# The first chunk of a latent projection on un-normed x, x read in two parts, modulation pieces in pairs

## The chip, the cores and the metric

The kernel runs on one core of one Trainium2 chip, in one launch. The metric is the device time of that launch in microseconds (us). Three runs of the kernel before took 2443.82, 2444.87 and 2444.91 us; the median, 2444.87 us, is the time before.

## The reference, cut to what matters

The program is one step of a two-layer trunk on 640 tokens (512 latent tokens from `x_sample`, 128 context tokens from `x_prompt`), each with 2048 features. The change lies in the first steps of the first layer, which compute this:

```python
def modulate_and_norm(x, cond, w_mod, b_mod, g):
    m = (jax.nn.silu(cond) @ w_mod + b_mod)[:, None, :]
    shift, scale, gate = jnp.split(m, 3, axis=-1)
    return rmsnorm(x, g) * (1 + scale) + shift, gate
...
h, g = modulate_and_norm(xp, cond_ctx, mod_w_ab[j], mod_b_ab[j], norm_ab[j])   # xs with c
...
q_lat, kv_lat, k_pe, a_gate, b_q, b_ff, b_fb, b_i, b_gate = split_cols(h @ w_in, AB_SIZES)
```

`rmsnorm(x, g)` is x · R · g, with R one number for each token: the inverse root of the mean square over all 2048 features. `w_mod` is 2048 x 6144 in float32, and of its columns shift takes 0 to 2047 and scale 2048 to 4095. Of `h @ w_in` the first stage computes the first 832 columns (the latent columns) and two gate blocks of 128.

## The kernel before

Activations stand transposed: features on the 128 partitions, the 640 tokens along the free axis, so 2048 features are 16 tiles, k = 0 to 15. TensorE (PE) multiplies float32 in three products: `split` makes a high and a low part of an operand (ACT writes the high part, DVE the low one), and `three` (lines 113 to 115) issues high·high, high·low and low·high.

The scheduler places every instruction by times of its own and writes one fixed order for each engine; an engine takes its instructions in that order and waits for semaphores. Nearly every DMA is issued by SyncE's queue (SP), also in one fixed order. It is the start stage (`run`, the block with the pool `start`) that the change rewrites:

- `conditioning` makes silu of the two conditions (`sc`).
- `read_x` reads the whole of x by rows of tokens: four tiles `x` of 128 tokens x 2048 (1 MB each), and the prompt in two tiles of the pool `rawp`. ACT squares each block of 512 for the sums of squares (line 372), PE transposes it in 128 x 128 blocks (line 48), and DVE copies the blocks to `xT`. For each group of 128 tokens, R is found and spread over the partitions by a small matmul (line 384).
- `start` needs scale and shift of tile k before it can build the operand `h[k]`. A column group j of `w_mod` (256 columns, thus two tiles k) is read as four pieces of 4 x 128 x 256 (512 KB each) into `rawp`; PE multiplies a piece in four column groups at a time (`mod_tensor`, line 269), then a copy (`modrow`) and a small matmul (line 277) put the result on the partitions. Block b needs the groups j = 8 + b (scale) and j = b (shift), so eight pieces and two small matmuls. All 16 groups (64 pieces, 33.6 MB) pass in this stage.
- `modulate(k)` multiplies tile k of `xT` by R (line 432), applies scale and shift (line 434) and splits the result into `act`.
- `columns(k0, k1, c)` multiplies a chunk of k tiles by column group c of `w_in_ab` (nine groups; a weight tile of two k is 128 KB), in two halves of 320 tokens, thus 12 matmuls for two k; the sums are gathered in `lat`, on ACT for the first chunk (line 411) and on DVE for the others (line 413). The chunks are k 0-1, 2-3, 4-7, 8-11 and 12-15, and while a chunk is multiplied, the pieces for the next chunks are multiplied between its matmuls.

`rawp` has four buffers, so that at most four pieces are loaded or loading. PSUM has four buffers `w` for transposes and small products, two `m` for the pieces and two `acc` for the matmuls of `columns`. In names as `raw_409` or `acc_521` the number tells tiles of one kind apart.

Of the kernel before, what the change touches and what calls it, by code (L numbers as in the profile page):

```python
# [14 lines left out]
P = 128  # L15
# [13 lines left out]
class Trunk:  # L29
# [229 lines left out]
    def mod_tensor(self, l, js):  # L259

        nc = self.nc
        wm = self.io[f"mod_w_{l}"][0].rearrange("(k p) c -> p k c", p=P)
        for j in js:
            ps = self.w("m")[:, :256]
            for kq in range(4):
                raw = self.t(self.rawp, [P, 4, 256], tag="raw")
                nc.sync.dma_start(raw, wm[:, 4 * kq:4 * kq + 4, 256 * j:256 * j + 256])
                for g in range(4):
                    nc.tensor.matmul(ps[32 * g:32 * g + 32, :], lhsT=self.sc[:, 4 * kq + g, :], rhs=raw[:, g, :],  # L269
                                     start=kq == 0, stop=kq == 3)  # L270
                if kq < 3:
                    yield
# [79 lines left out]
    def read_x(self, xin, sp):  # L352
# [4 lines left out]
        stats = []  # L357
        for i in range(5):
            if i < 4:
                x = self.t(xin, [P, D], tag="x", bufs=4)  # L360
                nc.sync.dma_start(x, io["x_sample"][0, P * i:P * i + P])
                blocks = [x[:, 512 * j:512 * j + 512] for j in range(4)]
            else:
                blocks = []
                for j in range(2):
                    x = self.t(self.rawp, [P, 1024], tag="raw")
                    nc.sync.dma_start(x, io["x_prompt"][0, :, 1024 * j:1024 * j + 1024])
                    blocks += [x[:, :512], x[:, 512:]]
            parts = self.t(sp, [P, 6], tag="parts", bufs=5)
            stats.append(parts)  # L370
            for j, x in enumerate(blocks):
                nc.scalar.activation(self.w("acc"), x, AF.Square, accum_out=parts[:, j:j + 1])
            for j, x in enumerate(blocks):
                p = self.w()
                for g in range(4):
                    self.transpose(p[:, P * g:P * g + P], x[:, P * g:P * g + P])
                nc.vector.tensor_copy(self.xblocks[j][:, :, P * i:P * i + P], p.rearrange("p (k t) -> p k t", t=P))
        for i, parts in enumerate(stats):
            r = self.t(sp, [P, 1], tag="r", bufs=2)
            nc.vector.reduce_sum(parts[:, 4:5], parts[:, 0:4], axis=AX.X)  # L380
            nc.vector.tensor_scalar(parts[:, 4:5], parts[:, 4:5], scalar1=1.0 / D, scalar2=None, op0=ALU.mult)
            self.rsqrt(r, parts[:, 4:5], parts[:, 5:6], EPS)
# [4 lines left out]
    def start(self):  # L387
        nc, io, sp = self.nc, self.io, self.startp
        self.h = []
        self.averages(sp, 1 / 512, 1 / 256)  # L390
        cols = [(P * c, P) for c in range(6)] + [(6 * P, 64)] + [(832 + P * h, P) for h in range(self.early)]
        sums = [self.t(sp, [P, T], tag="lat", bufs=len(cols)) for _ in cols]
        W = io["w_in_ab"][0].rearrange("(k p) c -> p k c", p=P)

        def columns(k0, k1, c):
# [3 lines left out]
            x = sums[c][:n]  # L399
            halves = [slice(HALF * h, HALF * h + HALF) for h in range(2)]  # L400
            done = []
            for s in halves:
                p = self.w("acc")[:n, :HALF]
                for k in range(k0, k1):
                    a = self.h[k]
                    self.three(p, (ws[:, 0, k - k0], ws[:, 1, k - k0]), (a[:, 0, s], a[:, 1, s]),
                               start=k == k0, stop=k == k1 - 1)
                done.append((s, p))
            for s, p in done:
                if k0 == 0:  # L410
# [17 lines left out]

        def modulate(k):
# [3 lines left out]
            for c, (s0, s1) in enumerate(((0, TS), (TS, T))):  # L433
                nc.vector.tensor_scalar(xn[:, s0:s1], xn[:, s0:s1], scalar1=self.mod["aba"][:, k, c:c + 1],
                                        scalar2=self.mod["ab"][:, k, c:c + 1], op0=ALU.mult, op1=ALU.add)
            a = self.t(self.act[k // 8], [P, 2, T + 2], F32R, tag="act")[:, :, 0:T]
            self.split(a[:, 0], a[:, 1], xn)
            self.h.append(a)

        work = []  # L440
        for b0, b1 in ((0, 1), (1, 2), (2, 4), (4, 6), (6, 8), (8, 8)):
            pieces = chain(*(self.mod_block(b, modulate) for b in range(b0, b1)))
            n = 8 * (b1 - b0)
            for j in range(4) if n == 0 else ():
                self.tc.keep_in_program_order(nc.sync.dma_start(
                    self.xT[4 * P * j:4 * P * (j + 1)].rearrange("(k p) t -> p k t", p=P), self.xblocks[j]))
# [6 lines left out]
            if b0 == 0:  # L453
                self.gains(sp)
            work = [lambda c=c, k0=2 * b0, k1=2 * b1: columns(k0, k1, c) for c in range(len(cols))]
# [505 lines left out]
    def out_ab(self, act, sp):  # L961
# [9 lines left out]
        for f in range(KT):  # L971
# [385 lines left out]
```

## Time and profile before

| | |
|---|---|
| runs | 2443.82, 2444.87, 2444.91 us (median 2444.87) |
| profiled execution | 2441.28 us, its span 2439.4 us, mean granted TensorE clock 0.995 |
| busy in the span | PE 2415.6 us (99%), DVE 1390.8 (57%), ACT 919.8 (38%), POOL 59.4 (2%) |
| DMA | 324.98 MB, 133 GB/s in the mean; 325 GB/s from 20 to 40 us |

The span runs from the first to the last instruction; the profiled execution's own time is 1.9 us longer and 3.6 us under the median. A busy PE is not PE at its peak: matmuls overlap, so the start of one after the other is the better measure of its pace. Instruction rows of the trace give start, length, engine, line, operation, output <- inputs and, in brackets, how long the engine stood idle before and what released it.

### The profile page before, as it was taken

The numbers are of one execution on the slowest core, as the hardware profiler recorded it, in microseconds if no ns is written. First come the engines' busy times: TensorE is split into PE (matmuls) and PEld (weight loads), VectorE is DVE, ScalarE is ACT, GpSimd is POOL, SyncE is SP. The second block draws the span as 40 slices with busy tenths as digits, with TensorE's granted clock in tenths as the row PEclk, the third lists the DMA queues.
The fourth block names the chain that finished last, engine by engine and source line by source line (L and its number), as shares of the span: only waits on it lengthen the run. The fifth ranks groups of instructions, "written<-read, shape, count | busy, mean of one in ns | idle before, by whom it ended". The sixth has DMA issues, their size and how long they took to land.

```text
span 2439.4 us, 42445 instructions
## 1 busy us (share of the span) xinstructions
PE 2415.6 (99%) x17418; PEld 2296.1 (94%) x17418; DVE 1390.8 (57%) x2874; ACT 919.8 (38%) x1717; POOL 59.4 (2%) x81
## 2 busy tenths in 40 slices
PE   7999999999999999999999999999999999999999
PEld 5789999999999999999999999999999999999999
DVE  5545455456455556566656668777765554654221
ACT  4314333333323333364544433443343443453121
POOL 1000000000000000000000121000000000000000
PEclk8999999999999999999999999999999999999999
DMA  9985544545545222453343655444432222225332
GB/s 313 307 260 153 168 146 149 164 132 164 157 126 153 71 65 73 137 147 92 91 118 107 192 170 160 128 118 123 132 115 72 75 81 78 74 66 162 115 113 61
DMA packets 396866, 324.98 MB, mean 133 GB/s; under 512 B 36250, under 2 KB 347968, under 8 KB 396160
## 3 DMA queue, kind: packets, MB, share of 16 engines
q1 hardware_dynamic: 396096, 322.17, 44.2%
q8 instruction: 137, 2.24, 0.4%
q0 software_dynamic: 576, 0.09, 0.1%
q14 instruction: 57, 0.47, 0.1%
HBM read 277.58 MB, written 36.76 MB: 129 GB/s over the span
## 4 chain that ended last, share of the span: by engine, by line
PE 95%; DMA 3%; DVE 1%; issue 0%; ACT 0%; SPq 0%; DVEq 0%; ACTq 0%
PE acc L113 25%; PE acc L115 24%; PE acc L114 24%; PE w L48 3%; PE o L1176 2%; PE m L292 2%; PE w L113 2%; PE w L115 2%; PE w L114 2%; DMA raw<-in_mod_w_ab_dram 1%; PE w L605 1%; PE m L269 1%; PE o L922 1%; PE w L636 1%; DMA raw<-in_w_in_ab_dram 1%; PE w L84 0%
## 5 line engine op out<-in xcount | busy, mean ns | idle before, releaser
L113 PE MATMUL acc<-act,split 128*128 128x320 f32 (+1 forms) x3552 | 1120.7, 316 | 3.8 <-ACT act L75 2.3
L114 PE MATMUL acc<-act,split 128*128 128x320 f32 (+1 forms) x3552 | 1109.1, 312 | 0.4 <-DVE act L76 0.3
L115 PE MATMUL acc<-act,split 128*128 128x320 f32 (+1 forms) x3552 | 1106.7, 312 | 0.3 <-DVE split L76 0.3
L113 PEld LDWEIGHTS acc<-act,split 128*128 128x128 f32 x3552 | 670.0, 189 | 47.6 <-issue 18.6
L114 PEld LDWEIGHTS acc<-act,split 128*128 128x128 f32 x3552 | 669.4, 188 | 5.4 <-DVE act L76 0.9
L115 PEld LDWEIGHTS acc<-act,split 128*128 128x128 f32 x3552 | 668.5, 188 | 4.7 <-issue 2.3
L75 ACT ACTIVATE split<-raw 128x1024 fp32r<-128x1024 f32 (+4 forms) x297 | 285.3, 961 | 696.5 <-PE acc L115 538.6
L76 DVE TENSOR_TENSOR split<-raw,split 128x1024 fp32r<-128x1024 f32 (+4 forms) x297 | 326.5, 1101 | 283.1 <-ACT split L75 277.7
L317 DVE SCALAR_TENSOR_TENSOR macc<-raw,sc,macc 128x512 f32<-128x512 f32 x120 | 86.0, 750 | 5.0 <-DMA raw<-in_mod_w_c_dram 5.0
L114 PE MATMUL acc<-mc,split 128*128 128x320 f32 x256 | 80.3, 314 | 0.1
L113 PE MATMUL acc<-mc,split 128*128 128x320 f32 x256 | 79.2, 314 | 0.2 <-ACT mc L75 0.2
L115 PE MATMUL acc<-mc,split 128*128 128x320 f32 x256 | 79.0, 309 | 0.0
L113 PE MATMUL acc<-mixa,split 128*128 128x320 f32 x256 | 78.8, 308 | 0.0
L114 PE MATMUL acc<-mixa,split 128*128 128x320 f32 x256 | 78.8, 308 | 0.0
L115 PE MATMUL acc<-mixa,split 128*128 128x320 f32 x256 | 78.7, 308 | 0.0
L577 DVE COPY_PREDICATED PS<-masks,w 128x384 f32<-128x384 uint8 x80 | 37.9, 516 | 67.8 <-PE w L605 47.7
L1159 ACT ACTIVATE sc<-sc,mxc,rqc 128x512 f32<-128x512 f32 (+2 forms) x80 | 56.0, 700 | 47.3 <-DVE mxc L1158 47.2
L413 DVE TENSOR_TENSOR lat<-lat,acc 128x320 f32<-128x320 f32 (+1 forms) x72 | 34.9, 485 | 58.3 <-PE acc L115 57.9
L1154 DVE CUSTOM_DVE_ANT_0 sc<-w,band 128x512 f32<-128x512 f32 (+2 forms) x80 | 43.5, 555 | 39.6 <-PE w L115 39.6
L951 DVE SCALAR_TENSOR_TENSOR y<-acc,mod_c,y 128x320 f32<-128x320 f32 (+2 forms) x48 | 19.5, 437 | 72.4 <-PE acc L115 72.4
L1176 PE MATMUL o<-pTc,vc 128*128 128x128 f32 x448 | 58.1, 275 | 0.0
L292 PE MATMUL m<-raw,sc 128*32 128x256 f32 x768 | 55.7, 386 | 0.0
(398 smaller groups left out, 3300.3 us busy)
## 6 DMA issues: line engine op xcount, KB each, us to landing
raw<-in_mod_w_ab_dram SPq DMA_DIRECT2D x96, 512.0 KB
raw<-in_mod_w_c_dram SPq DMA_DIRECT2D x96, 512.0 KB
raw<-in_w_in_ab_dram SPq DMA_DIRECT2D x92, 512.0 KB
raw<-in_w_in_c_dram SPq DMA_DIRECT2D x80, 512.0 KB
raw<-in_w_out_ab_dram SPq DMA_DIRECT2D x32, 512.0 KB
raw<-in_w_out_c_dram SPq DMA_DIRECT2D x32, 512.0 KB
raw<-in_w_in_ab_dram SPq DMA_DIRECT2D x24, 256.0 KB
xT<-xT SPq DMA_DIRECT2D x4, 1280.0 KB
```

What stands on the lines that cost most here:

```text
L48: self.nc.tensor.transpose(out, in_, self.ident[:k, :k])
L75: self.nc.scalar.activation(hi, full, AF.Copy)
L76: self.nc.vector.tensor_tensor(lo, full, hi.bitcast(F32), op=ALU.subtract)
L113: mm(out, lhsT=w[0], rhs=a[0], start=start, stop=False)
L114: mm(out, lhsT=w[0], rhs=a[1], start=False, stop=False)
L115: self.last = mm(out, lhsT=w[1], rhs=a[0], start=False, stop=stop).ins
L292: nc.tensor.matmul(ps[32 * g:32 * g + 32, :], lhsT=self.sc[:, k, :], rhs=raw[:, 256 * g:256 * g + 256], start=k == 0, stop=k == KT - 1)
L317: nc.vector.scalar_tensor_tensor(acc[:, c], raw[:, i], s, acc[:, c], op0=ALU.mult, op1=ALU.add)
L577: nc.vector.copy_predicated(dst[:, c0:c1], self.masks[:, mi].unsqueeze(1).to_broadcast([P, c1 - c0, P]), p[:, :P * (c1 - c0)].rearrange("p ...
L1154: nc.vector.tensor_tensor_reduce(s, in0=p, in1=self.band[:, m0:m0 + n], scale=1.0, scalar=-3e38, op0=ALU.add, op1=ALU.max, accum_out=mx[:, ...
L1159: nc.scalar.activation(s, s, AF.Exp, bias=mx[:, 2:3], scale=rq[:, b:b + 1], accum_out=mx[:, 0:1])
L1176: nc.tensor.matmul(od, lhsT=v[:, k0 // P + c], rhs=pT[:, c], start=c == 0, stop=c == nb - 1)
```

## The change

It does four things, all in the start stage.

- `read_first` reads only the first 256 features of x (five tiles `x0` of 128 KB), transposes them and squares them. `read_rest` reads the other 1792, one group of tokens at a time, between the column groups of the first chunk; the prompt's rest goes through two buffers of `rawp`. R is thus found within the first chunk.
- The first chunk (k 0-1) is multiplied on operands `z` (`raw_operand`, `shifted`) without R: x · g · (1 + scale), and two more columns in front that hold shift for the two conditions. The sums of `columns` (642 wide) are multiplied by R afterwards (nine DVE products, line 501 of the changed kernel), and the product of the shift columns is added in the next chunk's gathering. `modulate(0)` and `modulate(1)`, which later stages need, are done within a later chunk.
- The pieces of block 0 (groups 8 and 0) go to four buffers of `rawp`, then two in the pool `xin` (which has one buffer for them), then `rawp` again. `gains` comes after the first chunk.
- `mod_tensor` yields after every second piece instead of every piece, so that pieces come in pairs.

The diff, with the old `read_x` and the moved `shifted` left out (its body is the loop that stood in `out_ab`):

```diff
-    def mod_tensor(self, l, js):
+    def mod_tensor(self, l, js, pools=()):
...
+        pools = iter(pools)
         for j in js:
             ps = self.w("m")[:, :256]
             for kq in range(4):
-                raw = self.t(self.rawp, [P, 4, 256], tag="raw")
+                raw = self.t(next(pools, self.rawp), [P, 4, 256], tag="raw")
                 nc.sync.dma_start(raw, wm[:, 4 * kq:4 * kq + 4, 256 * j:256 * j + 256])
...
-                if kq < 3:
+                if kq == 1:
                     yield
...
+    def transposed(self, k0, x, i):
+
+        n = x.shape[1] // P
+        p = self.w()[:, :P * n]
+        for g in range(n):
+            self.transpose(p[:, P * g:P * g + P], x[:, P * g:P * g + P])
+        self.nc.vector.tensor_copy(self.xblocks[k0 // 4][:, k0 % 4:k0 % 4 + n, P * i:P * i + P],
+                                   p.rearrange("p (k t) -> p k t", t=P))
...
+        for i, rows in enumerate(self.xrows):
+            x = self.t(xin, [P, 2 * P], tag="x0", bufs=5)
+            nc.sync.dma_start(x, rows[:, 0:2 * P])
+            self.transposed(0, x, i)
+            self.squares(x, i, 0)
+
+    def read_rest(self, xin):
+
+        nc, sp = self.nc, self.startp
+        for i, rows in enumerate(self.xrows):
             if i < 4:
...
+                x = self.t(xin, [P, 14 * P], tag="x", bufs=4)
+                nc.sync.dma_start(x, rows[:, 2 * P:])
...
+                x, x2 = (self.t(self.rawp, [P, 1024], tag="raw") for _ in range(2))
+                nc.sync.dma_start(x[:, 0:768], rows[:, 256:1024])
+                nc.sync.dma_start(x2, rows[:, 1024:2048])
...
+            for j, (k0, a) in enumerate(parts):
+                self.transposed(k0, a, i)
+                self.squares(a, i, 1 + j)
+            yield
...
+                if extra:
+                    nc.scalar.activation(sums[c][:n, t0:t1], p, AF.Copy)
+                elif k0 == 2:
+                    for r, s0, s1 in self.REGIONS:
...
+                            nc.vector.scalar_tensor_tensor(x[:, s0:s1], p[:, s0 - t0:s1 - t0], sums[c][:n, r:r + 1],
+                                                           x[:, s0:s1], op0=ALU.add, op1=ALU.add)
...
+        for _ in self.mod_tensor("ab", (8, 0), [self.rawp] * 4 + [xin] * 2):
+            pass
+        z = [raw_operand(k) for k in (0, 1)]
+        rest = self.read_rest(xin)
+        pieces = self.mod_tensor("ab", (9, 1))
+        next(rest)
+        work = []
+        for c in range(len(cols)):
+            work.append(lambda c=c: columns(0, 2, c, z, 2))
+            if c < 5:
+                work.append(lambda: next(rest, None))
+        run(work[:-3], iter(()), 0)
+        run(work[-3:], pieces, 4)
+        for (_, n), x in zip(cols, sums):
+            nc.vector.tensor_tensor(x[:n, 2:], x[:n, 2:], self.R[:n], op=ALU.mult)
+        self.gains(xin)
+        yield
+        bounds = ((1, 2), (2, 4), (4, 6), (6, 8), (8, 8))
...
+            run(work, pieces, 4 * (b1 - b0))
+            if b0 == 1:
+                for k in (2, 3):
+                    modulate(k)
+            if b0 == 4:
+                for k in (0, 1):
+                    modulate(k)
```

What the change does to the fixed orders is seen at three places. On SP, up to the last piece of block 0, which is `raw_459` before: all of x has been issued ahead of these rows, and `raw_516` to `raw_660` are weight tiles of the first chunk.

```order
L100 DMA raw_516<-in_w_in_ab_dram 128x2x128
L100 DMA raw_544<-in_w_in_ab_dram 128x2x128
L100 DMA raw_571<-in_w_in_ab_dram 128x2x128
L267 DMA raw_421<-in_mod_w_ab_dram 128x4x256
L267 DMA raw_427<-in_mod_w_ab_dram 128x4x256
L267 DMA raw_441<-in_mod_w_ab_dram 128x4x256
L267 DMA raw_447<-in_mod_w_ab_dram 128x4x256
L100 DMA raw_598<-in_w_in_ab_dram 128x2x128
L100 DMA raw_632<-in_w_in_ab_dram 128x2x128
L100 DMA raw_660<-in_w_in_ab_dram 128x2x128
L267 DMA raw_453<-in_mod_w_ab_dram 128x4x256
L267 DMA raw_459<-in_mod_w_ab_dram 128x4x256
```

Now, on SP again: the five `x0` tiles and the pieces `raw_211` to `raw_243` stand ahead of these rows, and the last piece of block 0 to be issued is `raw_249`, a piece in the pool `xin`.

```order
L388 DMA x_287<-in_x_sample_dram 128x1792
L100 DMA raw_319<-in_w_in_ab_dram 128x2x128
L388 DMA x_340<-in_x_sample_dram 128x1792
L100 DMA raw_372<-in_w_in_ab_dram 128x2x128
L271 DMA raw_255<-in_mod_w_ab_dram 128x4x256
L388 DMA x_393<-in_x_sample_dram 128x1792
L100 DMA raw_425<-in_w_in_ab_dram 128x2x128
L271 DMA raw_261<-in_mod_w_ab_dram 128x4x256
L388 DMA x_446<-in_x_sample_dram 128x1792
L392 DMA raw_499<-in_x_prompt_dram 128x768
L393 DMA raw_500<-in_x_prompt_dram 128x1024
L271 DMA raw_249<-in_mod_w_ab_dram 128x4x256
```

So `raw_249` is now issued behind the whole of x, as the last piece of block 0 was before. On PE, where the first chunk is multiplied, before (`m` rows are pieces, `acc` rows the chunk's matmuls; all transposes of x stand ahead of them):

```order
L269 MATMUL m_653<-raw_654,sc_123 32x256 x4
L277 MATMUL w_627<-sel_380,modrow_625 128x2 x2
L269 MATMUL m_653<-raw_681,sc_123 32x256 x4
L113 MATMUL acc_549<-act_475,split_546 128x320
L114 MATMUL acc_549<-act_475,split_546 128x320
L115 MATMUL acc_549<-act_475,split_546 128x320
L113 MATMUL acc_549<-act_482,split_546 128x320
L114 MATMUL acc_549<-act_482,split_546 128x320
L115 MATMUL acc_549<-act_482,split_546 128x320
L269 MATMUL m_653<-raw_708,sc_123 32x256 x4
```

And now, at the second column group of the first chunk (`x_340` and `x_393` are two of the tiles of the rest of x):

```order
L48 MATMUL w_356<-ident_70,x_340 128x128 x4
L273 MATMUL m_637<-raw_671,sc_123 32x256 x4
L48 MATMUL w_364<-ident_70,x_340 128x128 x4
L113 MATMUL acc_377<-act_273,split_374 128x322
L114 MATMUL acc_377<-act_273,split_374 128x322
L115 MATMUL acc_377<-act_273,split_374 128x322
L113 MATMUL acc_377<-act_280,split_374 128x322
L114 MATMUL acc_377<-act_280,split_374 128x322
L115 MATMUL acc_377<-act_280,split_374 128x322
L48 MATMUL w_395<-ident_70,x_393 128x128 x2
L48 MATMUL w_401<-ident_70,x_393 128x128 x4
L273 MATMUL m_637<-raw_677,sc_123 32x256 x4
```

The transposes of the rest of x have moved between the matmuls of the first chunk. On PE, where the second chunk begins, before (`acc_759` is the last half of the first chunk, `acc_794` the first of the second):

```order
L113 MATMUL acc_759<-act_482,split_749 128x320
L114 MATMUL acc_759<-act_482,split_749 128x320
L115 MATMUL acc_759<-act_482,split_749 128x320
L269 MATMUL m_1038<-raw_1039,sc_123 32x256 x4
L113 MATMUL acc_794<-act_772,split_791 128x320
L114 MATMUL acc_794<-act_772,split_791 128x320
```

And now (`acc_754` is the last half of the first chunk, `acc_826` the first of the second):

```order
L115 MATMUL acc_754<-act_280,split_744 128x320
L281 MATMUL w_892<-sel_186,modrow_890 128x2 x2
L273 MATMUL m_919<-raw_960,sc_123 32x256 x4
L273 MATMUL m_1008<-raw_1009,sc_123 32x256 x4
L281 MATMUL w_968<-sel_186,modrow_966 128x2 x2
L273 MATMUL m_1008<-raw_1015,sc_123 32x256 x4
L273 MATMUL m_1008<-raw_1043,sc_123 32x256 x4
L273 MATMUL m_1008<-raw_1049,sc_123 32x256 x4
L281 MATMUL w_1057<-sel_186,modrow_1055 128x2 x2
L273 MATMUL m_1084<-raw_1085,sc_123 32x256 x4
L273 MATMUL m_1084<-raw_1091,sc_123 32x256 x4
L113 MATMUL acc_826<-act_811,split_823 128x320
```

Where one piece stood between the chunks, seven pieces and three small matmuls now stand with no other work beside them. The first matmul of the second chunk comes behind the 29th of the 64 pieces before, and behind the 30th now.

More of the change, by code (lines that the diff above doesn't have):

```diff
@@ L393, in start, with columns @@
         W = io["w_in_ab"][0].rearrange("(k p) c -> p k c", p=P)
-        def columns(k0, k1, c):
+        def columns(k0, k1, c, act, extra=0):
             c0, n = cols[c]
             ws = self.unit(W[:, k0:k1, c0:c0 + n], pool=sp, bufs=3)
-            x = sums[c][:n]
-            halves = [slice(HALF * h, HALF * h + HALF) for h in range(2)]
+            x = sums[c][:n, 2:]
+            cuts = ((0, HALF + extra), (HALF + extra, T + extra))
             done = []
-            for s in halves:
-                p = self.w("acc")[:n, :HALF]
+            for t0, t1 in cuts:
+                p = self.w("acc")[:n, :t1 - t0]
@@ L432, in modulate, with raw_operand, run @@
             nc.vector.tensor_tensor(xn, self.xblocks[k // 4][:, k % 4], self.R, op=ALU.mult)
-            for c, (s0, s1) in enumerate(((0, TS), (TS, T))):
+            for c, s0, s1 in self.REGIONS:
                 nc.vector.tensor_scalar(xn[:, s0:s1], xn[:, s0:s1], scalar1=self.mod["aba"][:, k, c:c + 1],
                                         scalar2=self.mod["ab"][:, k, c:c + 1], op0=ALU.mult, op1=ALU.add)
-            a = self.t(self.act[k // 8], [P, 2, T + 2], F32R, tag="act")[:, :, 0:T]
+            a = operand(k)[:, :, 0:T]
             self.split(a[:, 0], a[:, 1], xn)
[L438 to L446, printed above, removed]
+            self.h[k] = a
+        def raw_operand(k):
+            z = operand(k)
+            self.shifted(z, "ab", k, self.xblocks[k // 4][:, k % 4])
+            return z
+        def run(work, pieces, n):
             for i, w in enumerate(work):
@@ L452, in start @@
                 pass
[L453 to L455 removed]
+        for _ in self.mod_tensor("ab", (8, 0), [self.rawp] * 4 + [xin] * 2):
[16 more added lines that the diff above has]
+        bounds = ((1, 2), (2, 4), (4, 6), (6, 8), (8, 8))
+        for n, (b0, b1) in enumerate(bounds):
+            if b0 == 1:
+                work, pieces = [], iter(())
+            else:
+                pieces = chain(*(self.mod_block(b, modulate) for b in range(b0, b1)))
+            if b0 == 8:
+                for j in range(4):
+                    self.tc.keep_in_program_order(nc.sync.dma_start(
+                        self.xT[4 * P * j:4 * P * (j + 1)].rearrange("(k p) t -> p k t", p=P), self.xblocks[j]))
+            run(work, pieces, 4 * (b1 - b0))
+            if b0 == 1:
+                for k in (2, 3):
[3 more added lines that the diff above has]
+                    modulate(k)
+            work = [lambda c=c, k0=2 * b0, k1=2 * b1: columns(k0, k1, c, self.h) for c in range(len(cols))]
     def latent_norm(self, xs, j0, gain):
@@ L1205, in run @@
                 self.conditioning(xin)
-                self.read_x(xin, sp)
+                self.read_first(xin, sp)
                 self.parameters(xin)
+                steps = self.start(xin)
+                next(steps)
             late = ExitStack()
             self.act[1] = late.enter_context(pool("act1", "left", 8))
-            self.start()
+            for _ in steps:
+                pass
         with late:
```

82 lines of the change are left out of this document (37 added, 45 removed).

## The prediction

> **What bounds the kernel now.** I read the page's busy times and its chain first, then stretches of 20 us, then the chain and the instructions of the start stage.
>
> ```profile
> PE 2415.6 (99%) x17418; PEld 2296.1 (94%) x17418; DVE 1390.8 (57%) x2874; ACT 919.8 (38%) x1717; POOL 59.4 (2%) x81
> PE 95%; DMA 3%; DVE 1%; issue 0%; ACT 0%; SPq 0%; DVEq 0%; ACTq 0%
> ```
>
> PE carries 95% of the chain, so work added to PE lengthens the kernel, and only PE's waits can be shortened. In stretches (columns: PE, weight loads, DVE, ACT, POOL busy, then granted clock, DMA share, GB/s):
>
> ```profile
> 0.00:20.00 20.00, 10.95 (x70) 10.34 (x70) 10.23 (x29) 12.30 (x39) 11.32 (x37) 1.00 0.85 297
> 20.00:40.00 20.00, 15.72 (x114) 7.11 (x116) 9.42 (x37) 7.12 (x26) 0.00 (x0) 0.68 1.04 325
> 40.00:60.00 20.00, 20.00 (x164) 12.84 (x156) 11.18 (x29) 8.80 (x22) 0.00 (x0) 0.90 0.98 318
> 60.00:80.00 20.00, 20.00 (x175) 13.98 (x175) 9.35 (x23) 8.52 (x21) 0.00 (x0) 1.00 1.05 325
> 80.00:100.00 20.00, 20.00 (x175) 13.62 (x174) 15.10 (x37) 6.11 (x12) 0.00 (x0) 1.00 1.05 328
> 100.00:120.00 20.00, 19.66 (x153) 15.43 (x150) 10.56 (x23) 3.62 (x7) 0.00 (x0) 1.00 0.95 284
> ```
>
> Up to 40 us PE has room and DMA has none. From 40 to 100 us both are full: PE without a gap, DMA at about 325 GB/s. After that DMA has room and PE has none. So the only time to be won lies ahead of 41 us, and whatever is moved from there into 40 to 100 us is paid in full. The instructions at the two ends of the first chunk:
>
> ```profile
> 35.49 1.08 PE L269 MATMUL m<-raw,sc 128*32 128x256 f32 x8 [0.42 <-DMA raw<-in_mod_w_ab_dram]
> 37.07 1.08 PE L269 MATMUL m<-raw,sc 128*32 128x256 f32 x8 [0.49 <-DMA raw<-in_mod_w_ab_dram]
> 38.08 1.01 PE L277 MATMUL w<-sel,modrow 128*128 128x2 f32 x4
> 39.27 1.94 PE L269 MATMUL m<-raw,sc 128*32 128x256 f32 x16
> 41.13 0.90 PE L113 MATMUL acc<-act,split 128*128 128x320 f32 x2
> ...
> 72.89 0.64 PE L269 MATMUL m<-raw,sc 128*32 128x256 f32 x8
> 73.46 0.41 PE L113 MATMUL acc<-act,split 128*128 128x320 f32 x1
> 73.71 0.30 PE L114 MATMUL acc<-act,split 128*128 128x320 f32 x1
> ```
>
> The last piece of block 0 is multiplied at 35.49 us after a wait for its DMA; the first chunk begins at 41.13 us. By PE's order its 108 matmuls and 18 pieces later the second chunk begins, at 73.46 us: 32.33 us.
>
> **The change, part by part.** Its aim must be an earlier 41.13, and that needs the pieces of block 0 earlier. Bytes issued on SP up to the last of them: before, x (640 x 2048 x 4 = 5.24 MB), eight pieces of 0.524 MB and six weight tiles of 0.131 MB, 10.2 MB; now 0.66 MB of x0, eight pieces, three weight tiles and, because `raw_249` stands behind them, all 4.59 MB of the rest of x: 9.8 MB. That is 0.4 MB or 1.2 us less at 325 GB/s, so `raw_249` is there at about 34.3 us. Most of the early start has been lost in SP's order: `raw_249` needs the one buffer of `xin`, thus the end of `raw_243` on PE, and comes after four tiles and the prompt.
>
> Behind `raw_249` PE has three pieces (3 x 1.08; two stood there before, up to 38.08), the small matmul (1.01), ten transposes, and the piece `raw_638`. A piece in the chain (issued at 5.90 us behind all of x, it takes 17.18 us to land: the queue serves in order), a square, transposes and a lone transfer:
>
> ```profile
> 5.90 17.18 DMA raw<-in_mod_w_ab_dram
> ...
> 7.68 0.60 ACT L372 ACTIVATE acc<-x 128x512 f32<-128x512 f32 x1 [2.84 <-DMA x<-in_x_sample_dram]
> 7.70 6.47 PE L48 MATMUL w<-ident,x 128*128 128x128 f32 x32 [4.03 <-DMA x<-in_x_sample_dram]
> ...
> 15.18 1.94 PE L48 MATMUL w<-ident,x 128*128 128x128 f32 x16 [1.01 <-DMA x<-in_x_sample_dram]
> 21.90 0.49 PE L384 MATMUL w<-ident,r 128*128 128x128 f32 x2
> ...
> 0.74 0.39 SPq L157 DMA_DIRECT2D ident<-in_k_ident_dram  x1
> 3.35 0.18 PEld L48 LDWEIGHTS w<-ident,rowsc 32*128 32x128 f32 x1 [3.35 <-DMA ident<-in_k_ident_dram]
> ```
>
> At the slow pace of the 32 (0.20 us each) the ten take 2.0 us: 34.3 + 3.2 + 1.0 + 2.0 + 1.1 = 41.6 us. `raw_638` can be issued when `raw_255` is done, at 36.4 us; a lone DMA takes 2.6 us (0.74 to 3.35, 64 KB), and 0.46 MB more at 325 GB/s 1.4 us: there at 40.4 us, in time. Start: **+0.5 us**; ends -2 (all at the fast pace) and +3 (`raw_638` late).
>
> The pace hangs on PE's clock:
>
> ```profile
> 38.00:40.00 2.00, 2.00 (x17) 1.46 (x17) 0.79 (x4) 0.00 (x0) 0.00 (x0) 0.50 0.99 308
> 40.00:42.00 2.00, 2.00 (x18) 0.74 (x12) 1.97 (x8) 1.56 (x3) 0.00 (x0) 0.50 0.95 305
> 42.00:44.00 2.00, 2.00 (x13) 1.19 (x13) 2.00 (x5) 0.38 (x1) 0.00 (x0) 0.50 0.98 337
> 44.00:46.00 2.00, 2.00 (x19) 1.39 (x18) 1.01 (x5) 1.03 (x3) 0.00 (x0) 0.97 1.06 360
> ```
>
> Here six us of full PE pass at half clock before it is granted, so I take the slow pace up to the first chunk. The Trainium skill ("TensorE: Matmul & The Clock Gate", Part 1: The HAM clock gate) states that one busy window, about 3.4 us of sustained work, releases the clock. By that rule the ten transposes (0.12 us each) and the last piece (0.57) would run fast, and the sum below would be 1.3 us smaller. The trace does not bear it out here.
>
> Transposes moved. Of the rest of x, 70 transposes; ten stand ahead of the first chunk, 60 between its matmuls. At 1.94 / 16 = 0.12 us each: **+7.3 us**. Before, all 80 ran by 21.9 us in waits for x; now PE has no waits there unless the pieces are late, which is the rival of no change. R's five small matmuls go the same way: 5 x 0.49 = **+2.4 us**. Pieces: before, 11 of 64 were done at 41.13 us, now nine, so two more of the 64 lie behind:
>
> ```profile
> L269 PE MATMUL m<-raw,sc 128*32 128x256 f32 x152 | 13.0, 410 | 0.0
> 72.96 0.57 PE m L269 x8
> ```
>
> 2 x 0.57 = **+1.1 us**. No more changes of kind: a matmul of a chunk stands behind a piece or a transpose 60 times in the stage in both orders. The two columns more, 2 in 642, add 0.3% to 108 matmuls, under 0.1 us.
>
> The new joint. Between the chunks stand seven pieces and three small matmuls. PE needs 0.57 us for a piece, DMA 0.524 MB / 325 GB/s = 1.61 us, and at most four are ahead in `rawp`. During the first chunk PE uses 14 pieces in about 40 us (32.3, less four pieces, and the 9.7 of transposes and R), one every 2.8 us, so DMA idles there and can't make up for it. If three have landed, four wait 1.04 us each: **+4.2 us**; ends 0 and 7 x 1.04 = 7.3 us. In the second chunk 18 pieces stand where 15 stood: DMA needs 18 x 1.61 and nine weight tiles x 0.40 = 32.6 us, PE the 28.7 us of before (73.46 to 102.17, below) and 3 x 0.57 = 30.4: **+2.2 us**; ends 0 and 3. The three pieces come back later, since all 64 are needed anyway.
>
> ```profile
> 101.60 0.64 PE L269 MATMUL m<-raw,sc 128*32 128x256 f32 x8 [0.34 <-DMA raw<-in_mod_w_ab_dram]
> 102.17 0.41 PE L113 MATMUL acc<-act,split 128*128 128x320 f32 x1
> ```
>
> DVE at the joint: nine products of the sums with R, two `xn` products, scale and shift, then ACT and DVE split the first operand. The nearest rows:
>
> ```profile
> L432 DVE TENSOR_TENSOR xn<-xT,R 128x640 f32<-128x640 f32 x6 | 4.8, 810 | 0.0
> L434 DVE TENSOR_SCALAR xn<-xn,moda_ab,mod_ab 128x512 f32<-128x512 f32 (+1 forms) x8 | 3.0, 442 | 0.0
> L75 ACT ACTIVATE act<-xn 128x640 fp32r<-128x640 f32 x6 | 4.3, 736 | 4.2 <-DVE xn L434 4.2
> ```
>
> 11 x 0.81 + 2 x 0.44 + 0.74 = 10.5 us after the last of R. PE has, behind R's last matmul, 12 matmuls of the chunk (2.2 us), nine pieces (5.1) and five pairs of small matmuls (the pair took 1.01 us at half clock, so about 0.5 each, 2.5), 9.8 us without any wait. So the chain on DVE is covered by the waits for pieces, and if those were gone it would cost 0.7 us itself. The squares (20 now behind the first five, none over the 0.60 us of a 512-wide one) and `modulate(0)`, `modulate(1)` lie on ACT and DVE, 38% and 57% busy. `gains`, moved behind the chunk, was one transpose.
>
> Sum: 0.5 + 7.3 + 2.4 + 1.1 + 4.2 + 2.2 = 17.7 us. The profiled execution of 2441.28 us would become 2459.0; it lies 3.6 us under the median of 2444.87, on which the forecast stands: 2462.6, in round numbers **2462 us**, 0.7% slower. Nothing behind 200 us is changed but a few neighbours on PE near the first attention head, which I price at nothing, with 2 us either way in the range.
>
> **The rivals.** *No change: DMA sets the time of the second chunk anyway.* The bytes up to its first matmul are the same in both (29 or 30 pieces and x, 22 to 23 MB, which at 325 GB/s is the 73 us where it begins now), and DMA is full from 20 to 100 us. If the queue stayed full now too, the transposes would fall into waits that exist anyway, and the joint would cost nothing: 0 to 3 us, 2445 to 2448. Against it: a piece is issued only when PE frees a buffer, so PE's longer first chunk holds DMA back, and the prompt's rest holds two of the four buffers up to the end of its transposes.
>
> *Half hidden.* The waits at the joint (6.4 us) are there, but some of the transposes run while a piece is awaited: 6 to 10 us, 2451 to 2455.
>
> *Faster: the first chunk does begin early.* If `raw_249` came right behind `raw_243`, block 0 would be there after 0.66 + 4.19 MB, about 15 us of DMA behind 4 us, and the chunk could begin near 24 us; with 17 us won against the same 17.7 us, less the waits that an earlier chunk takes from the joint, some 6 us faster, 2439. It decides from the place of `raw_249`: it must not stand behind x. The fixed order puts it there, so this needs the queue to serve it out of order, against the 17.18 us of the piece above.
>
> *Slower still: the buffers.* The prompt's rest holds two of four buffers of `rawp` until PE's order has it transposed, late in the first chunk. If no piece of the seven has landed when PE arrives, and `raw_638` is late as well, joint, start and second chunk stand at their upper ends: 3.1 + 2.5 + 0.8 = 6.4 us more, 2469.
>
> **How the numbers follow.** The forecast's own case (2456 to 2468) has 0.66, half hidden 0.13, no change 0.11, faster 0.05, slower still 0.05. The range, 2450 to 2470, takes in the ends of start, joint and second chunk (-2 to +3, -4.2 to +3.1, -2.2 to +0.8) and the half-hidden case, and leaves 0.16 to no change and faster and a little above. A difference of 0.2% (4.9 us) is about what a measurement of this kernel tells from no change: faster 0.05, same 0.11, slower 0.84.
>
> **What would show it.** The first matmul on line 113 near 41 us and not near 24; the transposes of x, 60 of them, between 41 and 80 us; DMA well under 325 GB/s from 40 to 60 us; waits of line 273 for its pieces ahead of the second chunk, which begins near 90 us; the same distances from there on, so that the whole stage ends some 17 us later. I am wrong if the first chunk begins before 35 us, or if the second begins at 75.

## The result and the profile after

The changed kernel takes 2462.91 us (median of 4 runs, 2462.32 to 2464.0), the kernel before 2444.89 us beside it: 1.0079 times as long, 95% interval 1.0065 to 1.0092, thus 18.0 us slower. The forecast was 2462 us. The profiled execution took 2463.13 us with a span of 2461.4 us, near its median (that of before lies 3.6 us under its own).

The page after, its busy times and its chain:

```profile
PE 2419.5 (98%) x17418; PEld 2298.4 (93%) x17418; DVE 1402.6 (57%) x2903; ACT 924.4 (38%) x1733; POOL 59.3 (2%) x81
PE 92%; DMA 5%; DVE 1%; ACT 1%; SPq 1%; issue 0%; ACTq 0%; DVEq 0%
```

PE has the same count of matmuls, 17418; its share of the chain fell from 95% to 92%, and DMA's rose from 3% to 5%. PE's busy time grew by 3.9 us and the span by 22.0, so most of what was added is idle time of PE. Stretches of 20 us, with columns as before:

```profile
20.00:40.00 20.00, 5.13 (x35) 3.33 (x36) 2.79 (x7) 4.75 (x14) 0.00 (x0) 1.00 0.82 285
40.00:60.00 20.00, 20.00 (x157) 14.57 (x159) 13.36 (x40) 15.73 (x52) 0.00 (x0) 1.00 0.62 189
60.00:80.00 20.00, 20.00 (x175) 14.45 (x179) 10.37 (x32) 8.91 (x31) 0.00 (x0) 1.00 0.91 288
80.00:100.00 20.00, 16.54 (x142) 9.02 (x132) 17.41 (x46) 4.71 (x10) 0.00 (x0) 0.83 1.02 320
100.00:120.00 20.00, 18.54 (x166) 12.65 (x162) 16.25 (x40) 5.86 (x12) 0.00 (x0) 1.00 1.04 322
```

Before, PE was busy for 15.72 us from 20 to 40 us; now for 5.13. DMA, which gave 318 GB/s from 40 to 60 us, gives 189 there, and PE, which had no gap from 80 to 100 us, now stands for 3.5 us and runs part of the time at half clock. The places behind these numbers, on PE and (last two rows) in the chain and on SP's queue:

```profile
34.37 2.79 PE L273 MATMUL m<-raw,sc 128*32 128x256 f32 x24 [14.78 <-DMA raw<-in_mod_w_ab_dram]
38.53 2.38 PE L48 MATMUL w<-ident,x 128*128 128x128 f32 x10
41.79 0.42 PE L113 MATMUL acc<-act,split 128*128 128x322 f32 x1
...
82.76 0.64 PE L273 MATMUL m<-raw,sc 128*32 128x256 f32 x8 [0.87 <-DMA raw<-in_mod_w_ab_dram]
84.22 0.64 PE L273 MATMUL m<-raw,sc 128*32 128x256 f32 x8 [0.83 <-DMA raw<-in_mod_w_ab_dram]
85.43 0.61 PE L281 MATMUL w<-sel,modrow 128*128 128x2 f32 x4 [0.56 <-ACT modrow L278]
86.62 1.08 PE L273 MATMUL m<-raw,sc 128*32 128x256 f32 x8 [0.58 <-DMA raw<-in_mod_w_ab_dram]
88.02 1.08 PE L273 MATMUL m<-raw,sc 128*32 128x256 f32 x8 [0.32 <-DMA raw<-in_mod_w_ab_dram]
89.03 0.90 PE L113 MATMUL acc<-act,split 128*128 128x320 f32 x2
...
23.32 11.00 DMA raw<-in_mod_w_ab_dram
23.32 0.39 SPq L271 DMA_DIRECT2D raw<-in_mod_w_ab_dram  x1
```

`raw_249` is issued at 23.32 us, behind the prompt's rest, and PE waits 14.78 us for it. The first chunk begins at 41.79 us (41.13 before), the second at 89.03 (73.46 before) behind a row of seven pieces, four of which wait for DMA, the third at 123.1 (102.2 before). The difference is 20.9 us there, 17.5 us at 240 us and 17 to 22 at any later place.

### The profile page after: what moved, and what is told of

It reads as the page before. It is cut to its first block, busy times and chain, and to the rows that moved or that the text cites. A ratio compares the mean times of both kernels' runs of the same rounds, so it can differ in the third digit from the quotient of the medians.

```text
span 2461.4 us, 42501 instructions
## 1 busy us (share of the span) xinstructions
PE 2419.5 (98%) x17418; PEld 2298.4 (93%) x17418; DVE 1402.6 (57%) x2903; ACT 924.4 (38%) x1733; POOL 59.3 (2%) x81
## 4 chain that ended last, share of the span: by engine, by line
PE 92%; DMA 5%; DVE 1%; ACT 1%; SPq 1%; issue 0%; ACTq 0%; DVEq 0%
PE acc L113 24%; PE acc L115 23%; PE acc L114 23%; PE w L48 3%; PE o L1247 2%; PE w L113 2%; PE w L115 2%; PE w L114 2%; PE m L296 2%; DMA raw<-in_w_in_ab_dram 2%; PE w L671 1%; DMA raw<-in_mod_w_ab_dram 1%; PE m L273 1%; PE o L988 1%; PE w L702 1%; DMA y<-mixc 1%
## 5 line engine op out<-in xcount | busy, mean ns | idle before, releaser
L273 PE MATMUL m<-raw,sc 128*32 128x256 f32 x512 | 48.6, 435 | 21.7 <-DMA raw<-in_mod_w_ab_dram 21.5
L296 PE MATMUL m<-raw,sc 128*32 128x256 f32 x768 | 55.7, 386 | 0.0
```

## The experiments

Each was compared with runs of the kernel before on the same chip: e1 to e4 with 2442.39 us (median of 11 runs), e5 to e8 with 2441.75 us (15), e9 to e11 with 2441.76 us (19). The three columns in front are the starts of the first, second and third chunk in each trace. The profiled executions of e1, e5 and e11 were the slowest of their kernels' runs, so their traces show a little more than the medians.

| | first | second | third | median us | ratio to before |
|---|---|---|---|---|---|
| before | 41.1 | 73.5 | 102.2 | 2442.39, 2441.75, 2441.76 | |
| after | 41.8 | 89.0 | 123.1 | 2462.91 (before 2444.89) | 1.0079 (1.0065 to 1.0092) |
| e1 four pieces ahead | 26.8 | 73.3 | 112.2 | 2448.41 | 1.0025 (1.0015 to 1.0036) |
| e2 no transposes | 41.2 | 83.1 | 117.0 | 2452.94 | 1.0043 (1.0030 to 1.0055) |
| e3 single pieces | 41.6 | 88.8 | 122.3 | 2460.67 | 1.0076 (1.0063 to 1.0088) |
| e4 e1, POOL, early pieces | 25.0 | 67.1 | 105.4 | 2451.95 | 1.0040 (1.0027 to 1.0054) |
| e5 x ahead | 48.9 | 85.4 | 115.8 | 2450.00 | 1.0035 (1.0022 to 1.0047) |
| e6 prompt's own buffers | 40.8 | 89.1 | 125.4 | 2461.30 | 1.0080 (1.0066 to 1.0094) |
| e7 e1, early pieces | 26.0 | 72.8 | 107.9 | 2450.08 | 1.0034 (1.0022 to 1.0047) |
| e8 e7, lazy products | 26.1 | 73.7 | 106.2 | 2446.78 | 1.0023 (1.0015 to 1.0032) |
| e9 e5 and e6 | 48.3 | 78.5 | 108.5 | 2447.90 | 1.0026 (1.0016 to 1.0036) |
| e10 PE kept busy | 41.6 | 89.6 | 126.7 | 2464.09 | 1.0092 (1.0078 to 1.0106) |
| e11 e8, R first | 26.2 | 75.6 | 110.3 | 2445.65 | 1.0015 (1.0006 to 1.0024) |

**e1: the last pieces of block 0 ahead of the rest of x.** Its second four pieces get four buffers of `xin`, so that three of them, `raw_249` among these, move ahead of the rest of x, which has two buffers instead of four.

```diff
-raw = self.t(next(pools, self.rawp), [P, 4, 256], tag="raw")
+pool = next(pools, self.rawp)
+raw = self.t(pool, [P, 4, 256], tag="raw", bufs=None if pool is self.rawp else 4)
...
-x = self.t(xin, [P, 14 * P], tag="x", bufs=4)
+x = self.t(xin, [P, 14 * P], tag="x", bufs=2)
...
-for _ in self.mod_tensor("ab", (8, 0), [self.rawp] * 4 + [xin] * 2):
+for _ in self.mod_tensor("ab", (8, 0), [self.rawp] * 4 + [xin] * 4):
```

> The second group's four pieces get four buffers of xin (the rest of x two instead of four), so that raw_249 is issued ahead of the rest of x. Theory (the early start was lost in SP's order): 0.66 MB of x0, eight pieces and three weight tiles, 5.2 MB, stand ahead of the last piece of block 0, at the 272 to 285 GB/s of the first stretches 19 us behind the first 4; the first matmul of L113 starts near 24 us instead of 41.8, the second chunk between 68 and 76 instead of 89.0, and the kernel takes 2443 to 2450. Rival (DMA sets the second chunk, whenever the first begins): the first chunk begins early, but the second still at 85 or later, behind longer waits of L273, and the kernel takes 2458 to 2463. Rival (the first chunk then waits for x instead): the first matmul is near 24, but PE stands in waits of L48 for x between 25 and 50 us, second chunk near 80, 2452 to 2457.

On SP's queue the pieces now stand together, and PE begins the first chunk at 26.76 us:

```profile
4.95 10.03 SPq L272 DMA_DIRECT2D raw<-in_mod_w_ab_dram  x7
15.03 1.43 SPq L389 DMA_DIRECT2D x<-in_x_sample_dram  x1
...
26.76 0.62 PE L113 MATMUL acc<-act,split 128*128 128x322 f32 x1
...
73.25 0.88 PE L113 MATMUL acc<-act,split 128*128 128x320 f32 x2
```

The theory holds: the place of block 0's last pieces in SP's order costs 15.0 us at the first chunk, 15.8 at the second and 12 of the kernel's 18 us (2460.67 in e3, which is the changed kernel in all but names, to 2448.41: 12.3 us). It does not make the kernel faster than before, though. The prediction's rival that a start near 24 us would bring 6 us falls: with the start won, the second chunk begins only where it did in the kernel before, and the third comes 10 us late, since PE waits for pieces and runs at half clock around the joint. PE's waits from 27 to 93 us (3.0 of the 5.3 us at the joint, the longest, 1.7, within the second chunk), then two stretches:

```profile
PE m L274 <- DMA raw<-in_mod_w_ab_dram: 5.3, 8, 1.7
...
60.00:80.00 20.00, 16.85 (x130) 8.93 (x123) 17.39 (x41) 4.65 (x10) 0.00 (x0) 0.66 0.93 297
80.00:100.00 20.00, 18.27 (x127) 12.07 (x127) 12.26 (x30) 3.69 (x8) 0.00 (x0) 0.83 0.84 264
```

**e2: the moved transposes left out.**

```diff
 def transposed(self, k0, x, i):
     n = x.shape[1] // P
+    if k0 >= 2:
+        self.nc.vector.tensor_copy(self.xblocks[k0 // 4][:, k0 % 4:k0 % 4 + n, P * i:P * i + P],
+                                   x.rearrange("p (k t) -> p k t", t=P))
+        return
```

> Leaves out the transposes on PE of the features of x from 256 on (the copies on DVE stay, and put x untransposed into xT), so the outputs aren't the reference's. Theory (the moved transposes lie on PE's path between 41 and 80 us): 60 x 0.12 us = 7.3 us go, and up to 2 us of the ten ahead of the first chunk: first chunk at 40 to 41.8, second near 80 to 82, the kernel 2453 to 2456. Rival (DMA sets the time up to the second chunk): the transposes fell into waits that come anyway, the waits of L273 ahead of the second chunk grow by what goes, and the kernel takes 2460 to 2463. Between (half covered): 2457 to 2459.

The median is 7.7 us under e3's in the same comparison, the size that the theory gave. But in the traces the gain over e3 is 5.7 us at the second chunk and 4.0 at 240 us; the rest of it arises behind 1000 us, where both run the same instructions, and is not explained. So this run gives the transposes 4 to 6 us, not 7.7. Inside the chunk part of what they leave turns into waits (two stretches of e2, then PE's waits for pieces from 42 to 93 us, first in e2, then in the changed kernel):

```profile
40.00:60.00 20.00, 13.88 (x103) 8.64 (x104) 4.93 (x26) 14.94 (x56) 0.00 (x0) 0.88 0.75 236
60.00:80.00 20.00, 20.00 (x161) 14.46 (x160) 11.86 (x35) 8.05 (x25) 0.00 (x0) 0.95 0.90 282
...
PE m L273 <- DMA raw<-in_mod_w_ab_dram: 7.0, 6, 2.0
...
PE m L273 <- DMA raw<-in_mod_w_ab_dram: 2.6, 4, 0.9
```

Of e2's 7.0 us, 5.4 stand within the first chunk (47.7 to 58.0 us) and 1.6 within the second, none at the joint; the changed kernel's 2.6 all stand at the joint. PE also runs two stretches of the first chunk at half clock in e2 (41.38 to 44.80 and 58.45 to 61.86 us). So the transposes lie on PE's path, but without them PE waits in the chunk itself: the terms "transposes" and "joint" are not independent.

**e3: pairs undone.** `if kq == 1` back to `if kq < 3`, and the callers' counts doubled.

> The pairs alone undone: mod_tensor yields after every piece again, with the counts at its callers doubled. Theory: the order on each engine is the same, row by row, but for the numbers in names, so nothing changes: within 2 us of the changed kernel, 2461 to 2465. Rival (the pairs cost or bring something): more than 5 us off the changed kernel.

1.0076 against 1.0079: the pairs do nothing.

**e5 and e9: x ahead of the pieces again**, e9 with the prompt's rest in buffers of its own.

```diff
+for _ in self.read_rest(xin):
+    pass
 for _ in self.mod_tensor("ab", (8, 0), [self.rawp] * 4 + [xin] * 2):
     pass
...
-rest = self.read_rest(xin)
+rest = iter(())
...
-next(rest)
```

> Undoes one part: the rest of x is read, transposed and squared ahead of the pieces of block 0, as all of x was before; un-normed operands, the nine products by R, pairs and buffers stay. Theory (the 18 us come from where the rest of x stands: its transposes lose the waits that hid them, and DMA idles while PE does them): transposes and R are done by about 38 us again, first chunk at 41 to 44 us, second at 73 to 77, third at 102 to 106, the kernel 0 to 5 us over the kernel before. Rival (the un-normed operand with its nine products and the joint cost as much as the transposes): second chunk at 80 or later, kernel 8 to 14 us over the kernel before.

> e5 and e6 together: the rest of x ahead of the pieces of block 0, and the prompt's rest in two buffers of xin instead of two of rawp. Theory (in e5 the first chunk came at 48.9 us because the prompt's rest, transposed on PE only at 34.84 us, held two of four buffers of rawp, so that pieces came one at a time): pieces come from 18 us on without waits over 4 us, first chunk at 41 to 44, second at 71 to 76, third at 100 to 104, the kernel 0 to 5 us over the kernel before. Rival (something else in the changed order delays block 0): first chunk at 47 or later, the kernel 7 to 9 us over the kernel before.

e5 takes 8.2 us more than before and has its second chunk at 85.4 us, as its rival had it; e9 takes 6.1, between theory and rival. With un-normed operands, the nine products and the pairs all in place, putting the rest of x back regains 10 to 12 of the 18 us. That most of the loss hangs on where x stands is shown, by e1 from one side and by e5 and e9 from the other. What keeps e5 back is the start, 7.8 us late. Its prompt is transposed only at 34.84 us,

```profile
34.27 0.64 PE L273 MATMUL m<-raw,sc 128*32 128x256 f32 x8 [1.95 <-DMA raw<-in_mod_w_ab_dram]
34.84 1.75 PE L48 MATMUL w<-ident,raw 128*128 128x128 f32 x14
```

but buffers of its own (e9) bring the first chunk only from 48.9 to 48.3 us, so the theory on those falls. In both, the scheduler puts 13 or 14 pieces ahead of the first chunk, where 8 are needed and 11 stood before. Why it does so, and whether that is the cause, was not tried. In e9 the whole loss lies ahead of the first chunk: from there to the second it takes 30.2 us with 15 pieces, against 32.3 with 18 before, and three pieces are 1.7 us. So with x ahead the un-normed operand and its nine products cost next to nothing there, and the mechanism of e5's rival falls though its numbers came.

**e6: buffers for the prompt's rest alone.** `x, x2` in `xin` (tag `xp`, two buffers), the tiles `x` in three buffers.

> The prompt's rest gets two buffers of its own in xin (x three instead of four), so that rawp's four are free for pieces in the first chunk. Theory: PE's waits for pieces at the joint (2.6 us in the changed kernel's trace) go, but DVE's chain from the last R to the first operand (75.2 to 87.0 us) holds the second chunk at 87 or later; 1 to 4 us less than the changed kernel, 14 to 17 over the kernel before. Rival (the held buffers were a main cause): second chunk at 84 or earlier and 6 us or more less. Rival (they cost nothing): within 1 us of the changed kernel.

No gain: 1.0080 against 1.0076 to 1.0079. DMA does fill the first stretch and then idles in the next (the last row has PE's waits from 42 to 93 us):

```profile
40.00:60.00 20.00, 19.51 (x171) 14.32 (x164) 12.92 (x39) 17.03 (x55) 0.00 (x0) 1.00 0.95 302
60.00:80.00 20.00, 20.00 (x152) 14.90 (x150) 10.99 (x32) 8.23 (x28) 0.00 (x0) 1.00 0.65 203
...
PE m L273 <- DMA raw<-in_mod_w_ab_dram: 4.7, 4, 1.9
```

Of the 4.7 us, 4.2 stand at the joint, more than the 2.6 of the changed kernel. What comes early is lost again: from 40 to 80 us SP's queue waits 22.2 us, in 13 waits, for PE to be done with a piece, since PE's order takes pieces out of the buffers only at its own places for them. The prediction's "slower still" rival had given the held buffers a price; they have none here.

**e4, e7, e8, e11: what is left once the start is early.** All four are e1 with the pieces of block 1 spread over the whole first chunk. e4 puts the nine products on POOL, e7 leaves them on DVE, e8 moves them into the second chunk's gathering, e11 besides gives R and the operand of k 2 and 3 priority.

```diff
-run(work[:-3], iter(()), 0)
-run(work[-3:], pieces, 4)
+run(work, pieces, 4)
```

The nine products in e4, and in e8, where they go and this stands in `columns` for k0 == 2:

```diff
-nc.vector.tensor_tensor(x[:n, 2:], x[:n, 2:], self.R[:n], op=ALU.mult)
+nc.gpsimd.tensor_tensor(x[:n, 2:], x[:n, 2:], self.R[:n], op=ALU.mult)
...
+nc.vector.tensor_tensor(x[:, t0:t1], x[:, t0:t1], self.R[:n, t0:t1], op=ALU.mult)
```

> As e1, and besides the nine products of the sums with R on POOL instead of DVE, and the pieces of block 1 spread over the whole first chunk instead of its last three column groups. Theory (with the waits at the joint gone, the chain of DVE and the late pieces are what is left): second chunk between 60 and 68 us, the kernel 2440 to 2446, at or a little under the kernel before. Rival (POOL is slow: the nearest row of POOL, 128x640, takes 1.96 us, nine of them 17.6 us, against 7.3 on DVE): the second chunk's gatherings wait for POOL, PE waits for acc, and it is slower than e1 by 3 to 8 us. Rival (early pieces take DMA from x): waits of L48 for x within the first chunk, as slow as e1 or 2 us slower.

> As e4, but the nine products by R stay on DVE; against e4 only their engine differs, against e1 only the pieces of block 1, spread over the first chunk. Theory (in e4 POOL's products slowed DVE: its 128x640 products took 1.8 to 1.9 us each beside POOL and 0.81 alone): behind the last R near 60 us the chain on DVE takes 10.5 us, second chunk's matmuls run from 70 to 71 us without the 5.5 us wait of e4, third chunk at 101 to 104, the kernel 3 to 6 us under e4, thus 2 to 6 over the kernel before. Rival (POOL did no harm): within 2 us of e4 or slower.

> As e7, but the sums are multiplied by R half by half where the second chunk's sums are added to them (18 DVE products of half the size instead of nine ahead of the chunk). Theory: the chain at the joint is 7.3 us shorter, so the second chunk can begin near 66 us, when block 1's modulation is done, and the kernel is 2 to 5 us under e7, level with the kernel before or a little under it (-3 to +2 us). Rival (DMA, not DVE, sets what follows): second chunk earlier, but third at the same time as in e7, within 1 us of e7. Rival (the products still stand ahead of the first operand in DVE's order): no change at the second chunk either.

> As e8, with the finding of R and the modulation of k 2 and 3 given a higher priority in the scheduler. Theory (in e8 the last R, at 64.14 us on PE, waited for DVE's lazy products, and so did the operand of the second chunk, ready at 72.9 us): the last R comes at 60 to 61, the operand at 68 to 70, the second chunk 2 to 4 us earlier than 73.7, the kernel 1 to 3 us under e8. Rival (pieces for later chunks stand ahead of the second chunk in PE's order, and their DMA sets its start): within 1 us of e8.

Spreading block 1's pieces brings nothing that the measurement tells from e1 (1.0034 against 1.0025). POOL took 1.48 us for a product, less than the nearest row had let expect (1.96), and slowed DVE. Groups of e4 at the joint (the first row from 59.7 to 66.2 us, the others from 58 to 76), then the same on DVE in e7:

```profile
L465 DVE TENSOR_TENSOR xn<-xT,R 128x640 f32<-128x640 f32 x2 | 3.8, 1884 | 0.0
L467 DVE TENSOR_SCALAR xn<-xn,moda_ab,mod_ab 128x512 f32<-128x512 f32 x2 | 3.1, 1540 | 0.0
L501 POOL TENSOR_TENSOR lat<-lat,R 128x640 f32<-128x640 f32 x8 | 11.6, 1483 | 43.7 <-ACT R L407 43.7
...
L465 DVE TENSOR_TENSOR xn<-xT,R 128x640 f32<-128x640 f32 x4 | 3.0, 796 | 0.0
L467 DVE TENSOR_SCALAR xn<-xn,moda_ab,mod_ab 128x512 f32<-128x512 f32 x4 | 2.1, 535 | 0.0
```

PE then waited 5.5 us for the operand within e4's second chunk, yet e4's third chunk came earlier than e7's, and the two times can't be told apart (1.0040 and 1.0034), as e7's rival had it: the slower DVE is shown, a cost to the kernel is not. Taking the products off the chain (e8) did not bring the second chunk forward: 73.7 us against 72.8, not the 66 of the theory. In PE's order 26 pieces stand ahead of it where blocks 0 and 1 need 16. The others are for later chunks, some stand ahead of the last R too, and these wait for DMA:

```profile
61.71 0.64 PE L274 MATMUL m<-raw,sc 128*32 128x256 f32 x8 [1.51 <-DMA raw<-in_mod_w_ab_dram]
63.58 0.64 PE L274 MATMUL m<-raw,sc 128*32 128x256 f32 x8 [1.23 <-DMA raw<-in_mod_w_ab_dram]
64.14 0.49 PE L406 MATMUL w<-ident,r 128*128 128x128 f32 x2
...
66.41 1.08 PE L274 MATMUL m<-raw,sc 128*32 128x256 f32 x8 [0.60 <-DMA raw<-in_mod_w_ab_dram]
```

e11, with priority for R, has its last R at 66.90 us, behind a piece that waited 3.36 us. So its theory falls; the time is 1.1 us under e8's, which the intervals don't separate, about what the rival had. That the pieces in PE's order set the joint is read from these waits; no run moved them. e11 has the lowest time of all, 3.9 us or 0.15% (0.06 to 0.24%) over the kernel before; none is under it.

**e10: PE kept busy at the joint.**

```diff
+if l == "ab" and 23 <= self.npiece < 29:
+    d = self.w()[:, :256]
+    for g in range(4):
+        nc.tensor.matmul(d[32 * g:32 * g + 32, :], lhsT=self.sc[:, 4 * kq + g, :], rhs=raw[:, g, :],
+                         start=True, stop=True)
```

> The changed kernel, with the matmuls of six pieces at the joint issued a second time into an unused PSUM buffer, so that PE stands idle less. Theory (the half clock from 86.04 to 92.87 us follows the stretch of 3.41 us ahead of it, in which PE was busy for only 1.89 us): the clock stays full or the half clock is a window shorter, second chunk at 88 to 89, third at 119.5 to 121 instead of 123.1, the kernel 2 to 4 us under the changed kernel, 14 to 16 over the kernel before. Rival (the half clock has another cause): half clock as before, 6 x 0.57 = 3.4 us of matmuls partly on top, 0 to 3 us over the changed kernel. Rival (the clock stays full, but DMA or DVE sets what follows): second chunk earlier by under 1 us, third within 1 us of the changed kernel's.

At the joint the drop to half clock comes one stretch later and lasts one stretch of 3.41 us instead of two. But a second drop follows from 123.52 to 126.94 us, ahead of the third chunk (last row). Columns as in the stretches above, first the changed kernel, then e10:

```profile
82.63:86.04 3.41, 1.89 (x20) 0.84 (x20) 3.07 (x11) 1.05 (x3) 0.00 (x0) 1.00 1.04 306
86.04:89.45 3.41, 2.51 (x17) 0.85 (x18) 3.38 (x10) 0.69 (x2) 0.00 (x0) 0.50 1.09 363
89.45:92.87 3.42, 3.42 (x17) 2.28 (x17) 1.58 (x6) 0.74 (x1) 0.00 (x0) 0.50 1.09 338
...
82.56:85.98 3.42, 2.35 (x38) 1.02 (x34) 3.02 (x12) 0.62 (x2) 0.00 (x0) 1.00 0.91 282
85.98:89.39 3.41, 1.91 (x28) 0.91 (x28) 2.95 (x7) 1.12 (x3) 0.00 (x0) 1.00 0.99 324
89.39:92.80 3.41, 3.41 (x22) 2.31 (x16) 1.12 (x4) 0.00 (x0) 0.00 (x0) 0.50 1.08 347
...
120.00:140.00 20.00, 17.91 (x137) 13.66 (x133) 12.65 (x29) 4.38 (x9) 0.00 (x0) 0.91 0.82 247
```

That fits the theory on what makes the clock drop (1.89 and 1.91 us busy in the stretch ahead, 1.32 ahead of the second drop, while 2.35 did not do it here, though 2.34 did in e9), but no time was won: second chunk at 89.6, third at 126.7, the kernel 3.4 us over e3, with intervals that overlap. Both kernels spend 6.83 us of this stage at half clock, so the run doesn't show what the half clock costs. The second chunk still waits for its pieces, whichever clock PE has.

## Why the prediction was right

- *Start, +0.5.* 41.13 became 41.79: +0.7. `raw_249` was awaited until 34.37 us (forecast 34.3), the ten transposes took 2.38 us (2.0), the last piece 1.02 (1.1). The slow pace was right here: the trace's first record of a granted clock is at 41.67 us. Ahead of it the column shows 1.00 for want of a record, but a piece takes 1.08 us there and 0.64 behind it. e1 shows the cause, the place in SP's order.
- *First chunk, transposes 7.3, R 2.4, pieces 1.1, joint 4.2, in sum 15.0.* From the first chunk to the second it takes 47.2 us against 32.3, thus 14.9 more. The parts fit less well than their sum, so that its closeness is partly luck. Counted from the start of each matmul to the start of the next, with waits apart, the 60 transposes take 6.7 us and R 1.1. The waits at the joint are 2.6 us for DMA and 0.56 for `modrow`, 3.2 where 4.2 stood. Pieces and small matmuls take 5.0 us more instead of 1.1: three pieces more lie between the chunks (21 for 18), not two, and two of them run at half clock (1.08 for 0.64), which the prediction did not foresee. The chunk's own matmuls take 1.3 us less, since before they began at half clock. R's five small matmuls, priced at 0.49 each from a row of before that had been measured in waits, run in the chunk's stream at about half of it (the next instruction starts 0.22 us later):

```profile
74.10 0.38 PE L405 MATMUL w<-ident,r 128*128 128x128 f32 x2
74.32 0.95 PE L281 MATMUL w<-sel,modrow 128*128 128x2 f32 x8
```

  e2 adds that transposes and waits trade against each other: without the one, the other grows by 4.4 us up to 93 us.
- *Second chunk, +2.2.* 34.0 us against 28.7: +5.3, at the third chunk. By the fourth (170.4 against 152.7 us, +17.7) 3.2 us have come back; the prediction had said so of three pieces (1.7), and four fewer stand in the third chunk (16 for 20). So +2.2 was about right for what stays; that it would be 5.3 for a while, at half clock and with waits, was not foreseen.
- *DVE's chain, covered.* It was put at 10.5 us behind R. R's last matmul is at 74.10 us, and the first half of the operand is split on DVE by 87.0 us, 12.9 us later, 2 us ahead of the second chunk. Covered, but by less than was said; in e8, without the nine products ahead of it, the second chunk still waits behind its pieces.
- *The rivals.* "No change" falls: DMA did not stay full (189 GB/s from 40 to 60 us). But it and "half hidden" are right in a part, since in e2 4.4 us of waits came in place of the transposes it saved. "Faster" was wrong twice: `raw_249` stands behind x, and where it does not (e1), the result is 6 us slower than before and not 6 us faster. Its step "less the waits that an earlier chunk takes from the joint" failed: PE waits 3.0 us there for pieces in e1, where the changed kernel has 2.6, then 1.7 within the second chunk, and it spends 20.5 us at half clock instead of 6.8. "Slower still" falls with e6.

Left open: 6 to 8 us remain in e9 and e5 with x put back, what the half clock costs, and the scheduler's order of pieces ahead of the first chunk and at the joint, which was seen in the traces but not changed.

## What to carry to other kernels

Where PE and DMA are both full, a step moved out of an earlier wait is paid for the most part (5.7 us at the second chunk for 60 transposes), and the gain of moving it depends on the place of the last transfers it needs in a queue that serves in order: look up what stands ahead of the last transfer that the early start needs, in bytes, before anything else. When that was mended here, the traces point at the order on PE as the next limit, though no run changed it: work that only later stages need, placed ahead of the stage on hand, makes PE wait for transfers, and two more buffers did not help (e6). Price moved work and the waits behind it together, since each hides the other.

## What the runs showed of the hardware

- The granted clock changes in stretches of 3.41 us: in this stage it was half for 6.83 us in the changed kernel (86.04 to 92.87), 13.65 and again 6.83 in e1, 10.24 in e8, twice 3.41 in e10. In the rows above it fell behind a stretch with PE busy for 1.89 or 1.91 of 3.41 us and came back behind a full one. Before, it took two full stretches (first two rows), and in e8 a stretch of 1.90 us was passed and only the next one, of 2.19, was followed by the drop (last two), so busy time alone does not settle it:

```profile
37.29:40.71 3.42, 3.42 (x29) 1.65 (x21) 1.50 (x6) 0.40 (x1) 0.00 (x0) 0.50 1.00 318
40.71:44.12 3.41, 3.41 (x22) 1.85 (x15) 3.38 (x9) 1.54 (x4) 0.00 (x0) 0.50 0.96 323
...
58.59:62.00 3.41, 1.90 (x28) 0.77 (x26) 3.38 (x12) 0.74 (x2) 0.00 (x0) 1.00 1.02 304
62.00:65.42 3.42, 2.19 (x26) 1.41 (x19) 0.69 (x3) 0.66 (x2) 0.00 (x0) 1.00 0.99 305
```

  The Trainium skill ("TensorE: Matmul & The Clock Gate", Part 1: The HAM clock gate) says that a free-running window of 3413 ns decides. The lengths agree with it, and so do the places: the drops of the changed kernel at 86.04, 1089.56 and 1133.93 us lie 294 and 13 times 3413 ns apart. The prediction's sentence that the trace does not bear out the rule went too far: one full window was enough in the changed kernel (89.45 to 92.87), two were needed before. The traces hold a difference that no run varied: of the full stretches after a drop in this stage, the seven that no grant followed (37.29 to 40.71 before, five more in e1, e5, e6 and e7, one in e11) hold 0.57 to 1.87 us of the small 128x2 matmuls, those followed by a grant at most 0.16; the full stretch ahead of e7's first grant held 0.61. The Trainium skill has the clock drop after an idle window; here stretches in which PE was busy for 39% (e5) to 71% (e7) were followed by a drop.
- While POOL multiplied two tiles of SBUF, DVE's 128x640 product of two such tiles took 1.88 us (the first two in e4). Behind POOL's last product, at 72.77 us, the next two took 0.81 and 0.76, and e7 without POOL has 0.80. ACT's split of 128x640 kept its 0.74 us. The Trainium skill ("SBUF — State Buffer", SBUF: two separate sides) says that the two engines share a port pair that one instruction holds for its whole length. The slowdown of DVE agrees; for how long the pair is held no run here shows.
